# The first k-tile without its norm and shift, and two k-tiles' modulation sums on VectorE, in a two-branch transformer layer

## Chip, cores and metric

The kernel runs on one core of a Trainium2 chip. The metric is the device time of one execution in microseconds; the number given for a kernel is the median of several runs. Profiles are taken of one further execution, whose span is the time from its first to its last instruction.

TensorE multiplies, VectorE and ScalarE do element-wise work, GpSimd (POOL) here mostly issues DMAs, and SyncE (SP) issues nearly all loads. Each engine, and each queue of DMA issues, works through its own list in order.

## The reference, cut to what matters

One layer over 128 context and 256 latent tokens (384 together, three tiles of 128), with a model width of 2048 (16 k-tiles of 128 channels), all in float32:

```python
def modulation(cond, w_mod, b_mod):
    m = jax.nn.silu(cond) @ w_mod + b_mod          # 2048 -> 6 * 2048
    return jnp.split(m[..., None, :], 6, axis=-1)  # sh1, sc1, g1, sh2, sc2, g2

h = rms_norm(x, n1) * (1 + sc1) + sh1
p = h @ w_in                                       # 2048 -> 4096: q, k, v, u
...
x = x + g1 * token_mixing(h, attn, u, ...)         # h again, for the gates
h2 = rms_norm(x, n2) * (1 + sc2) + sh2
x = x + g2 * swiglu(h2, w_gate_up, w_down)
```

Context tokens have one condition vector, latent tokens another, so each channel has two shifts and two scales. The change touches only the way from x to `h @ w_in`.

## The kernel before

**Products.** A float32 product is made of three: each operand is split into a rounded high part H (ScalarE) and the rest L (VectorE), and TensorE adds H·H, L·H and H·L in PSUM. `unit` does so for two k-tiles of a weight chunk of 512 columns (lines 170, 171, 176), and `next_unit` splits the next unit's weights beforehand and then steps the side jobs. A side job is a generator behind a `Paced` object, which takes so many steps per unit as its rate says.

**Input projection.** It needs all 16 k-tiles of h, and each needs its modulation sums, 2.1 MB of weights per k-tile. So it is done in four groups of k-tiles (`GROUPS`): k-tile 0; 1 and 2; 3 to 6; 7 to 15. Each group runs over all eight chunks of 512 columns (`ORDER`), with one accumulator `acc` in SBUF per chunk, to which the later groups are added (`done`, line 783). Group 0 is 24 blocks (eight chunks by three token tiles), with an explicit table `opening_jobs` of what is put beside which block.

**Opening.** The tokens are loaded first, transposed on TensorE (`turn`, line 511), squared on ScalarE; `roots` makes 1/rms from the sums and a row `rB` of it over all partitions. After the tokens come k-tile 0's modulation weights (four loads, lines 419 and 436), then the first weight units. Only when the norm, the scale and the shift are there does `opening_high` make k-tile 0's operand.

**Modulation sums.** `mod_sums` multiplies SiLU(cond) with shift and scale weights, four small products side by side in TensorE's columns (line 436), eight steps per entry (first k-tile, count) of `MODS`, four for a single k-tile. `mod_cols` turns the result (line 452) and makes shift and scale columns; `modulate` makes a k-tile's H and L (scale and shift on ScalarE). `prepare` does this for all entries in turn, paced by `PREP` and `DUE` per group. The weights go through four buffers `wm`, the projection's through four buffers `raw`; both are issued on SP's queue when a buffer is free. `scale` multiplies the other k-tiles by `rB`, one per unit.

**Later.** When `prepare` is done, `with_rows` gives its memory to the modulation rows of the second half, which VectorE sums (line 363) beside the products.

PSUM has four tiles for products in groups 0 to 2 (`ps`) and four for the rest (`pa`); a block or a unit's three token tiles take one each.

## Time and profile before

| | us |
|---|---|
| median of 3 runs (2005.52 to 2007.36) | 2006.64 |
| the profiled execution | 2005.29 |
| its span | 2003.5 |
| TensorE busy | 1989.5 (99% of the span) |
| VectorE busy | 1226.0 (61%) |
| ScalarE busy | 718.3 (36%) |
| first product of the projection (k-tile 0) | starts at 19.66 |
| first product of k-tiles 1 and 2 | starts at 44.82 |
| first product of k-tiles 3 to 6 | starts at 88.56 |
| first product of k-tiles 7 to 15 | starts at 173.53 |

A row of a timeline has the start, the length, the engine, the line and operation, the output and inputs with their shapes, how many instructions were merged, and in brackets how long the engine was idle before and what ended that. Products overlap: one of 512 columns is listed with 0.39 us, but the next starts 0.23 later. A float32 product that is not split is two records in the trace. Rows of groups have minimum, median and maximum of one instruction in ns. Rows of DMA issues have the count, the size of one and the median time from issue to landing.

### The profile page before, as it was taken

What the parts mean: (1) busy time and instruction counts of PE and PEld (TensorE: products, weight loads), DVE (VectorE), ACT (ScalarE), POOL (GpSimd) and SP (SyncE); (2) the same over time, 40 slices, a digit from 0 to 9 for tenths busy, and PEclk for the clock granted to TensorE, in tenths of its full rate; (3) what the DMA queues carried; (4) which work ended last, traced back from release to release, by engine and by line L of the source; (5) the groups of instructions that cost most, each with busy time, mean ns of one, the idle gap of its engine ahead of it and who ended that gap; (6) DMA issues with size and microseconds to landing.
All of it is one profiled execution on the core that took longest, in us unless ns stands there. A gap on an engine that the chain in (4) does not pass through costs nothing.

```text
span 2003.5 us, 24190 instructions
## 1 busy us (share of the span) xinstructions
PE 1989.5 (99%) x9404; PEld 1628.4 (81%) x9404; DVE 1226.0 (61%) x1493; ACT 718.3 (36%) x1052; POOL 73.9 (4%) x106
## 2 busy tenths in 40 slices
PE   8999999999999999999999999999999999999999
PEld 5767888887777888889988888888888888888887
DVE  6745999879877886776843454554334433434654
ACT  6324332445554443344423322323232233223231
POOL 0000010101010100100001000001000000000000
PEclk9999999999999999999999999999999999999999
DMA  9896898888886898764457464547444544455463
GB/s 347 289 342 206 308 288 312 271 278 283 269 255 216 284 330 264 252 231 131 134 182 200 158 189 164 188 139 211 137 150 129 165 153 131 132 152 174 158 185 104
DMA packets 140658, 425.28 MB, mean 212 GB/s; under 512 B 17856, under 2 KB 39296, under 8 KB 139520
## 3 DMA queue, kind: packets, MB, share of 16 engines
q1 hardware_dynamic: 127344, 400.51, 60.4%
q0 software_dynamic: 9600, 16.88, 3.9%
q10 hardware_dynamic: 3600, 6.34, 0.9%
q8 instruction: 74, 1.21, 0.2%
q14 instruction: 40, 0.33, 0.0%
HBM read 387.50 MB, written 44.63 MB: 216 GB/s over the span
## 4 chain that ended last, share of the span: by engine, by line
PE 95%; DMA 2%; DVE 2%; ACT 1%; issue 1%; SPq 0%; DVEq 0%; ACTq 0%
PE mm L170 19%; PE mm L176 18%; PE mm L171 18%; PE at L170 10%; PE at L171 10%; PE at L176 10%; PE at L436 1%; DMA wm<-in_w_mod 1%; PE at L1039 1%; PE at L977 1%; PE at L1056 1%; DVE wl L156 1%; PE at L1447 1%; PE at L1453 1%; PE mm L1453 1%; PE mm L1447 1%
## 5 line engine op out<-in xcount | busy, mean ns | idle before, releaser
L156 DVE TENSOR_TENSOR wl<-wraw,wh 128x1024 fp32r<-128x1024 f32 (+1 forms) x464 | 553.7, 1202 | 435.1 <-ACT wh L155 251.7
L155 ACT CAST wh<-wraw 128x1024 fp32r<-128x1024 f32 (+1 forms) x464 | 478.5, 1038 | 757.9 <-PE mm L171 454.1
L170 PE MATMUL mm<-wh,hH 128*128 128x512 f32 x1316 | 518.2, 394 | 0.3 <-ACT hH L155 0.3
L171 PE MATMUL mm<-wh,hL 128*128 128x512 f32 x1316 | 513.2, 390 | 0.2
L176 PE MATMUL mm<-wl,hH 128*128 128x512 f32 x1316 | 357.2, 389 | 0.2 <-DVE wl L156 0.2
L363 DVE SCALAR_TENSOR_TENSOR accr<-wmr,csz,accr 128x1024 f32<-128x1024 f32 x240 | 301.6, 1278 | 4.6 <-DMA wmr<-in_w_rows 4.6
L170 PEld LDWEIGHTS mm<-wh,hH 128*128 128x128 f32 x1316 | 247.0, 188 | 65.6 <-issue 12.7
L176 PEld LDWEIGHTS mm<-wl,hH 128*128 128x128 f32 x1316 | 246.9, 188 | 52.2 <-DVE wl L156 0.6
L171 PEld LDWEIGHTS mm<-wh,hL 128*128 128x128 f32 x1316 | 247.2, 188 | 50.6 <-DVE hL L156 0.8
L170 PE MATMUL at<-wh,hH 128*128 128x512 f32 x616 | 240.1, 390 | 0.0
L171 PE MATMUL at<-wh,hL 128*128 128x512 f32 x616 | 239.7, 389 | 0.0
L176 PE MATMUL at<-wl,hH 128*128 128x512 f32 x616 | 169.4, 389 | 0.0
L176 PEld LDWEIGHTS at<-wl,hH 128*128 128x128 f32 x616 | 115.6, 188 | 24.0
L171 PEld LDWEIGHTS at<-wh,hL 128*128 128x128 f32 x616 | 115.7, 188 | 23.9
L170 PEld LDWEIGHTS at<-wh,hH 128*128 128x128 f32 x616 | 115.6, 188 | 23.9
L170 PE MATMUL mm<-wh,cH 128*128 128x512 f32 x278 | 108.1, 389 | 0.0
L171 PE MATMUL mm<-wh,cL 128*128 128x512 f32 x278 | 108.1, 389 | 0.0
L176 PE MATMUL mm<-wl,cH 128*128 128x512 f32 x278 | 76.6, 389 | 0.0
L170 PE MATMUL at<-wh,cH 128*128 128x512 f32 x196 | 76.2, 389 | 0.0
L171 PE MATMUL at<-wh,cL 128*128 128x512 f32 x196 | 76.2, 389 | 0.0
L783 DVE TENSOR_TENSOR acc<-acc,mm 128x512 f32<-128x512 f32 x60 | 40.4, 685 | 43.8 <-PE mm L176 43.8
L171 PEld LDWEIGHTS mm<-wh,cL 128*128 128x128 f32 x278 | 52.2, 188 | 10.8
(287 smaller groups left out, 1817.1 us busy)
## 6 DMA issues: line engine op xcount, KB each, us to landing
wraw<-in_w_gate_up SPq DMA_DIRECT2D x176, 512.0 KB, 3.8
wmr<-in_w_rows SPq DMA_DIRECT2D x128, 512.0 KB, 5.2
wraw<-in_w_down SPq DMA_DIRECT2D x88, 512.0 KB, 3.9
wraw<-in_w_gate SPq DMA_DIRECT2D x64, 512.0 KB, 5.0
wraw<-in_w_in SPq DMA_DIRECT2D x60, 512.0 KB, 5.6
wm<-in_w_mod SPq DMA_DIRECT2D x24, 768.0 KB, 6.1
wraw<-in_w_o SPq DMA_DIRECT2D x32, 512.0 KB, 6.2
wm<-in_w_mod SPq DMA_DIRECT2D x28, 512.0 KB, 6.1
```

The source lines that it names most:

```text
L155: nc.scalar.copy(H, x)
L156: nc.vector.tensor_sub(L, x, fr(H))
L170: nc.tensor.matmul(po[t], H[k0 + i][:, sl], wH[:, i], start=first and i == 0, stop=False)
L171: nc.tensor.matmul(po[t], L[k0 + i][:, sl], wH[:, i], start=False, stop=False)
L176: nc.tensor.matmul(po[t], H[k0 + i][:, sl], wL[:, i], start=False, stop=last and i == n - 1)
L363: nc.vector.scalar_tensor_tensor(out=acc[:, cnd], in0=wm, scalar=sc, in1=acc[:, cnd], op0=ALU.mult, op1=ALU.add)
L436: nc.tensor.matmul(pm[q : q + 32, :w], csz[:, k, :], wm[:, kk + par, ty, :], start=k < 2, stop=k >= KT - 2, tile_position=(0, q), skip_gro ...
L783: nc.vector.tensor_add(a, a, po[t])
L977: nc.tensor.matmul(po[j][:, cols], t["q"][rows[j], q], t["k"][rows[j], k], start=True, stop=True, tile_position=(j * HD, 0),)
L1039: nc.tensor.transpose(o[:, i * P : (i + 1) * P], sc[:, j, c0 : c0 + P], ident)
L1447: nc.tensor.matmul(o, a, xH, start=u + kk == 0, stop=False)
L1453: nc.tensor.matmul(o, a, wide(u + kk)[0], start=False, stop=last and kk == 1)
```

## The change

1. *Opening.* The tokens come turned from the host's layout (`x_turned`), so no transposes. First on SP's queue stand the scale half of k-tile 0's weights, that k-tile's tokens and the first two weight units; the shift half and the other tokens follow. Here are rows of SP's queue, before from the eleventh load on, now from the first (`xc`, `xT`: tokens; `wm`: modulation weights; `wraw`: weights of the projection):

```order
L484 DMA xc_133<-in_x_in 128x512
L484 DMA xc_134<-in_x_in 128x512
L419 DMA wm_151<-in_w_mod 128x1024
L419 DMA wm_153<-in_w_mod 128x1024
L419 DMA wm_155<-in_w_mod 128x1024
L419 DMA wm_157<-in_w_mod 128x1024
L228 DMA wraw_159<-in_w_in 128x2x512
```

```order
L490 DMA wm_137<-in_w_mod 128x1024
L490 DMA wm_138<-in_w_mod 128x1024
L485 DMA xT_133<-in_x_turned 128x384
L229 DMA wraw_142<-in_w_in 128x512 x2
L229 DMA wraw_145<-in_w_in 128x512 x2
L490 DMA wm_148<-in_w_mod 128x1024
L490 DMA wm_149<-in_w_mod 128x1024
L485 DMA xT_133<-in_x_turned 128x1152
L485 DMA xT_134<-in_x_turned 128x1536
L229 DMA wraw_154<-in_w_in 128x512 x2
L485 DMA xT_135<-in_x_turned 128x1536
L485 DMA xT_136<-in_x_turned 128x1536
```

Twelve token loads headed the queue before, then k-tile 0's weights; now two loads of scale weights do, and the last tokens are the fourteenth and fifteenth load.

2. *Group 0* multiplies `x * scale` of k-tile 0, not normed and not shifted. When group 1 is added, the accumulator is multiplied by 1/rms per token (`r1`, line 960). The shift's part is a row per condition, shift times weights (`shift_rows`), written to DRAM and, in group 2, loaded to all partitions and added (`shifted`). The operand of k-tile 0 that the gates need later is made at the end of group 2. The squares are summed beside group 0's blocks: ScalarE squares three quarters, VectorE one and folds the others in (`squares`, `fold`), TensorE sums over the partitions (`square_sums`). On TensorE's queue, blocks 15 to 19 now read (`mm`: a block's products; `at`: side work; `sqx`: squares; `ssr`: their sums):

```order
L863 MATMUL mm_379<-wh_338,hH_24_225 128x512
L864 MATMUL mm_379<-wh_338,hL_25_226 128x512
L865 MATMUL mm_379<-wl_339,hH_24_225 128x512
L437 MATMUL at_384<-wm_162,csz 32x256 x4
L863 MATMUL mm_392<-wh_338,hH_24_225 128x512
L864 MATMUL mm_392<-wh_338,hL_25_226 128x512
L865 MATMUL mm_392<-wl_339,hH_24_225 128x512
L437 MATMUL at_384<-wm_164,csz 32x256 x4
L863 MATMUL mm_406<-wh_338,hH_24_225 128x512
L864 MATMUL mm_406<-wh_338,hL_25_226 128x512
L865 MATMUL mm_406<-wl_339,hH_24_225 128x512
L564 MATMUL at_411<-sqx_131,ones 32x384 x4
```

The first step for k-tiles 1 and 2 stood after block 3 before and stands after block 15 now, the square sums after block 17; the eighth step comes after block 21, where it came after block 16; the transposes that follow it came after block 18 and come after block 22 now.

3. *K-tiles 14 and 15.* `MODS` ends at k-tile 13. `last_columns` sums the other two on VectorE: sixteen loads on GpSimd's queue into one buffer, each followed by two passes (line 715), at 0.95 per unit from group 1 on; then one product against ones, a way through DRAM to turn it, and `modulate`. VectorE's queue in group 1, before and now (`acc`: accumulators, `wl`: split weights, `total`: the new sums, `wml`: their weights):

```order
L156 TENSOR_TENSOR wl_692<-wraw_513,wh_691 128x1024
L539 TENSOR_TENSOR xT_136<-xT_136,rB_168 128x384
L783 TENSOR_TENSOR acc_366<-acc_366,mm_688 128x512
L783 TENSOR_TENSOR acc_366<-acc_366,mm_689 128x512
L783 TENSOR_TENSOR acc_366<-acc_366,mm_690 128x512
```

```order
L157 TENSOR_TENSOR wl_696<-wraw_547,wh_695 128x1024
L630 TENSOR_TENSOR xT_134<-xT_134,rB_173 128x384
L715 SCALAR_TENSOR_TENSOR total<-wml_667,csz,total 128x512 x2
L960 SCALAR_TENSOR_TENSOR acc_240<-acc_240,r_172,mm_692 128x512
L960 SCALAR_TENSOR_TENSOR acc_240<-acc_240,r_172,mm_693 128x512
L960 SCALAR_TENSOR_TENSOR acc_240<-acc_240,r_172,mm_694 128x512
```

Two passes that read a loaded buffer now stand ahead of each unit's accumulations.

4. *Pace.* `DUE` and `PREP` for groups 1 and 2 are other numbers, and `prepare` and the shift adds are run to their end where group 3 begins, so `with_rows` comes there.

```diff
-MODS = [(0, 1), (1, 2), (3, 2), (5, 2), (7, 3), (10, 3), (13, 3)]
+MODS = [(0, 1), (1, 2), (3, 2), (5, 2), (7, 3), (10, 3), (13, 1)]
+LAST = (14, 2)
-DUE = [-1.4, 0, 0, 0]
-PREP = [1.75, 2.5, 1.8, 1.8]
+DUE = [-1.4, -1, 0.4, 0]
+PREP = [1.75, 2.8, 1.6, 1.8]
...
-            for t in range(NT):
-                load_tokens(t)
+            wm_scale = load_first(1)
+            load_tokens(0, 0, 1)
+            loads = Ahead(load_unit, units, 2)
+            wm_shift = load_first(0)
+            load_tokens(0, 1, 4)
+            load_tokens(1)
+            loads.more()
+            load_tokens(2)
+            load_tokens(3)
+            loads.more()
             for _ in range(4):
                 src.more()
...
+            def squares(cc):
+                if cc:
+                    nc.scalar.activation(out=sq[1], in_=xT[cc], func=AF.Square)
+                else:
+                    nc.vector.tensor_mul(sq[0], xT[0], xT[0])
+            def fold():
+                nc.vector.tensor_add(sq[0], sq[0], sq[1])
...
+            def shift_rows(j):
+                o = at_tile()
+                for g in range(4):
+                    nc.tensor.matmul(
+                        o[32 * g : 32 * g + 32], sh0, opened[2 * j + g // 2][0][:, g % 2],
+                        start=True, stop=True, tile_position=(0, 32 * g), skip_group_check=True,
+                    )
+                row = tmp.tile([P, CH], F32, tag="junk", bufs=1, name=nm("srow"))
+                nc.scalar.copy(row, o)
+                for g in range(4):
+                    nc.gpsimd.dma_start(s_shift[j][2 * g : 2 * g + 2], row[32 * g : 32 * g + 2])
...
+            def last_columns():
...
+                def load(k):
+                    wm = tmp.tile([P, 2 * n * P], F32, tag="junk", bufs=1, name=nm("wml"))
+                    nc.gpsimd.dma_start(wm, io[f"w_mod{kt0}"][:, k].rearrange("p i n -> p (i n)"))
+                    return wm
+                wm = load(0)
+                yield
+                for k in range(KT):
+                    for cnd in range(2):
+                        a, sc = total[:, cnd], csz[:, k, cnd : cnd + 1]
...
+                            nc.vector.scalar_tensor_tensor(
+                                out=a, in0=wm, scalar=sc, in1=a, op0=ALU.mult, op1=ALU.add
+                            )
+                    if k < KT - 1:
+                        wm = load(k + 1)
+                    yield
...
+            last = Paced(last_columns(), 0.95)
...
             def opening_high():
                 for c, sl in conds2:
-                    nc.vector.tensor_scalar(
-                        h0H[:, sl], xT[0][:, 0, sl], msc[0][:, 0, c : c + 1], msh[0][:, 0, c : c + 1],
-                        op0=ALU.mult, op1=ALU.add,
-                    )
+                    nc.vector.tensor_scalar_mul(h0H[:, sl], xT[0][:, 0, sl], msc[0][:, 0, c : c + 1])
...
             opening_jobs = [
                 (1, 1, lambda: open_pair(1, 0)),
                 (3, 1, lambda: open_pair(1, 1)),
+                (4, 1, shift_sums),
+                (5, 1, warm_sqrt),
+                (6, 1, shift_columns),
+                (7, 1, lambda: squares(0)),
+                (8, 1, lambda: shift_rows(0)),
...
+                (12, 1, fold),
...
+                (14, 1, fold),
+                (15, 1, step),
+                (15, 1, lambda: squares(3)),
...
+                (16, 1, fold),
+                (16, 1, step),
+                (17, 1, square_sums),
...
+                (21, 2, step),
+                (22, 3, step),
+                (23, 2, step),
...
                         def done(t):
                             a = acc[ci][:, t]
-                            nc.vector.tensor_add(a, a, po[t])
+                            if gi > 1:
+                                nc.vector.tensor_add(a, a, po[t])
+                                return
+                            nc.vector.scalar_tensor_tensor(
+                                out=a, in0=a, scalar=r1[:, t : t + 1], in1=po[t], op0=ALU.mult, op1=ALU.add
+                            )
```

More of the change, by code (lines that the diff above doesn't have):

```diff
@@ L516, in square @@
-            def square(t, cc):
-                junk = tmp.tile([P, CH], F32, tag="junk", bufs=1, name=nm("junk"))
-                nc.scalar.activation(
-                    out=junk, in_=xc[cc][:, t], func=AF.Square, accum_out=ssx[:, t, cc : cc + 1]
-                )
+            pick = tmp.tile([P, 2], F32, tag="pick", bufs=1, name="pick")
+            nc.vector.tensor_reduce(
+                out=pick, in_=ident.rearrange("p (a c) -> p c a", c=32)[:, 0:2], axis=AX.X, op=ALU.add
+            )
@@ new lines, in picked @@
+            def picked(o, mrow, w=P):
+                for t in range(w // P):
+                    nc.tensor.matmul(
+                        o[:, 2 * t : 2 * t + 2], mrow[:, t * P : (t + 1) * P], pick, start=True, stop=True
+                    )
+                return o[:, : 2 * (w // P)]
+            def squares(cc):
[3 more added lines that the diff above has]
+                    nc.vector.tensor_mul(sq[0], xT[0], xT[0])
@@ new lines, in fold, with square_sums @@
+            def fold():
+                nc.vector.tensor_add(sq[0], sq[0], sq[1])
+            norm = {}
+            def square_sums():
+                pm = at_tile()
+                for k in range(4):
+                    q = 32 * k
+                    nc.tensor.matmul(
+                        pm[q : q + 32, :TOK], ones, sq[0][:, k], start=True, stop=True,
+                        tile_position=(0, q), skip_group_check=True,
+                    )
+                norm["row"] = tmp.tile([P, CH], F32, tag="junk", bufs=1, name=nm("ssr"))
+                nc.scalar.copy(norm["row"][:, :TOK], pm[:, :TOK])
@@ L522, in roots, with roots_row @@
             def roots():
-                nc.vector.tensor_reduce(out=ss1, in_=ssx, axis=AX.X, op=ALU.add)
-                for _ in inv_sqrt(r1, ss1, D, [P, NT]):
+                ss = picked(at_tile(), norm["row"], TOK).rearrange("p (t c) -> p t c", c=2)[:, :, 0]
+                for _ in inv_sqrt(r1, ss, D, [P, NT]):
                     pass
+            def roots_row():
                 o = at_tile()
@@ L572, in trunk_kernel @@
             sums = []
-            for i, _ in enumerate(mod_sums(src, *MODS[0], wme, sums)):
-                if i == 5:
-                    roots()
-                    unread(1)
-            unread(2)
-            loads.more()
-            loads.more()
-            prepared = [1]
-            cols = mod_cols(*MODS[0], sums.pop())
-            next(cols)
-            unread(5)
-            for _ in cols:
-                pass
+            prepared = [1]
+            unread(10)
+            o = picked(at_tile(), first_sums(wm_scale, 3))
+            unread(3)
+            nc.vector.scalar_tensor_tensor(
+                out=msc[0][:, 0], in0=o, scalar=b0[:, 0:1], in1=ng[:, 0, 0:1].to_broadcast([P, 2]),
+                op0=ALU.add, op1=ALU.mult,
+            )
             def columns_and_tokens(k0, n):
@@ L648, in open_pair @@
                 split(H[:, j], L[:, j], raw[:, j])
-                if j:
-                    loads.more()
             opening_high()
@@ L729, in with_rows @@
                 behind.append(rows)
-            prep.then = with_rows
-            behind += [scales, prep]
+            behind += [scales, prep, last]
             def after(ci):
@@ L768, in trunk_kernel @@
                 prep.least = 3.6 if gi > 1 else 1
+                if gi == 2:
+                    shift = Paced(shifted())
+                    behind.append(shift)
                 if gi == len(GROUPS) - 1:
+                    shift.drain()
+                    behind.remove(shift)
+                    prep.drain()
+                    with_rows()
+                    last.rate = 1
                     behind.append(Paced(head_constants(), 0.2))
```

173 lines of the change are left out of this document (130 added, 43 removed).

## The prediction

> **What bounds the kernel now.** I read the page's busy lines first, then the chain, then what TensorE waited for in the first 200 us, because every edited line runs before 180 us.
>
> ```profile
> PE 1989.5 (99%) x9404; PEld 1628.4 (81%) x9404; DVE 1226.0 (61%) x1493; ACT 718.3 (36%) x1052; POOL 73.9 (4%) x106
> PE 95%; DMA 2%; DVE 2%; ACT 1%; issue 1%; SPq 0%; DVEq 0%; ACTq 0%
> PE at L511 <- DMA xc<-in_x_in: 3.8, 1, 3.8
> PE at L436 <- DMA wm<-in_w_mod: 3.1, 5, 0.7
> PE mm L170 <- ACT hH L155: 0.3, 1, 0.3
> ```
>
> TensorE is the bound from end to end. Time can be won in two ways only: its first product starts earlier, or it gets less to do. Either counts only if nothing that feeds it becomes late. Now the opening (timelines; the columns are start, length, engine, line):
>
> ```profile
> 3.82 2.79 PE L511 MATMUL at<-ident,xc 128*128 128x128 f32 x12 [3.82 <-DMA xc<-in_x_in]
> 6.42 0.63 ACT L518 ACTIVATE junk<-xc 128x512 f32<-128x512 f32 x1 [0.18 <-DMA xc<-in_x_in]
> 13.40 0.65 PE L436 MATMUL at<-wm,csz 128*32 128x128 f32 x16 [0.65 <-DMA wm<-in_w_mod]
> 17.14 0.64 PE L436 MATMUL at<-wm,csz 128*32 128x128 f32 x16
> 17.72 0.71 PE L570 MATMUL mm<-ident 128*128 128x128 f32 x4
> 17.86 0.27 ACT L444 COPY mrow<-at 128x128 f32<-128x128 f32 x1 [0.36 <-PE at L436]
> 19.16 0.67 DVE L623 TENSOR_SCALAR hH<-xT,ms 128x128 fp32r<-128x128 f32 x2
> 19.66 1.03 PE L689 MATMUL mm<-wh,hH 128*128 128x512 f32 x3
> 10.00:20.00 10.00, 7.94 (x102) 5.78 (x102) 6.35 (x19) 7.01 (x18) 0.00 (x0) 1.00 1.04 404
> 20.00:30.00 10.00, 10.00 (x63) 5.78 (x63) 6.83 (x12) 5.67 (x11) 0.00 (x0) 1.00 1.03 401
> ```
>
> The reader should see that the first real product waits until 19.66 for bytes: 3.1 MB of tokens and 2.1 MB of modulation weights at about 400 GB/s. The rows also give a landing curve: the fourth quarter-MB (1.05 MB) is there at 6.42, 3.67 MB at 13.40, and from there 0.40 MB per us.
>
> **The change, part by part.** *Start.* Only the scale half of k-tile 0's weights (1.05 MB) stands ahead of the first product. It lands at about 6.4 by the curve. Then come half of L436's last 32 records (0.6; 16 cost 0.64), and the way from their end (17.72, where L570 starts) to the product at 19.66, which is 1.9, less two of three small VectorE steps (0.2 each): 1.55. First product at 8.5, so 11.1 us earlier.
>
> *What k-tile 0's blocks then carry.* The prices, and the block's end before:
>
> ```profile
> 30.66 0.39 PE L696 MATMUL mm<-wh,hH 128*128 128x512 f32 x1
> 31.35 0.39 PE L696 MATMUL mm<-wh,hH 128*128 128x512 f32 x1
> 32.83 0.64 PE L436 MATMUL at<-wm,csz 128*32 128x256 f32 x8 [0.63 <-DMA wm<-in_w_mod]
> 33.40 0.50 PE L696 MATMUL mm<-wh,hH 128*128 128x512 f32 x1
> 39.99 0.38 PE L452 MATMUL at<-ident,mrow 128*128 128x128 f32 x2
> 43.74 1.07 PE L436 MATMUL at<-wm,csz 128*32 128x256 f32 x16
> 44.26 0.51 ACT L155 CAST hH<-hf 128x384 fp32r<-128x384 f32 x1
> 44.82 0.50 PE L170 MATMUL mm<-wh,hH 128*128 128x512 f32 x1
> ```
>
> A block of three products is 0.69 us, so 24 are 16.5, and 0.3 more for the first three. Nine modulation steps (eight records of 256 columns, 0.6 each) are 5.4, transposes 0.3. New on TensorE: the shift sums, 32 records, two times 0.6 = 1.2; the two shift rows, each eight records of 512 columns, twice the 256-column step, 1.0 each = 2.0; the square sums (384 columns) 0.75; picks and the transposes of r 0.5. That is 4.4 us of new work which stood under the loads before or did not exist. Without waits the first product of k-tiles 1 and 2 would come at 8.5 + 16.8 + 5.4 + 0.3 + 4.4 = 35.4.
>
> *Waits there.* Three, each from a queue. (1) The first weights of k-tiles 1 and 2 now stand behind 7.3 MB on SP's queue and end at 7.86 MB: 13.4 + 4.19/0.40 = 23.8, while TensorE has block 15 behind it at 8.5 + 0.3 + 16 x 0.69 + 1.2 + 1.0 = 22: 1.9 us. (2) The squares. A VectorE pass over 128x1536 is taken as 1.75 us, from 128x512 at 0.68 and 128x1024 at 1.22:
>
> ```profile
> L156 DVE TENSOR_TENSOR wl<-wraw,wh x35: 681/1219/1226, 19.7 to 175.5; 128x1024 fp32r<-128x1024 f32 x27, 128x512 fp32r<-128x512 f32 x8
> ```
>
> From block 7's end (8.5 + 0.3 + 8 x 0.69 + 1.2 = 15.5) VectorE has one square and three folds (7.0), four splits (about 2.6) and five accumulator copies (0.6 to 0.7 each), and it runs through them back to back to 28.2; the sums over them are reached by TensorE at 23.8 + 2 x 0.6 + 2 x 0.69 = 26.4: 1.8 us. (3) The weights of steps 6 to 8 have their buffers free only as steps 2 to 4 end, some 0.4. And k-tiles 1 and 2 become operands late: transposes, three small steps, scaling and rounding need at least 2.7 us from transpose to product, and only one block and one step (1.3) stand between them now, where five blocks and two steps stood (39.99 to 44.82): 1.1 us rounded down. Together 5.2. Bounds: 0, if the loads come at a higher rate from the first byte (they also shorten VectorE's queue), and 9, if (1) and (2) add up with later loads. I take 5.2, the queue as it stands.
>
> So k-tiles 1 and 2 start at 40.6 instead of 44.82, with one step fewer behind them (0.6): 3.6 us won, not 11.1.
>
> *K-tiles 14 and 15.* The later stretches start and end here:
>
> ```profile
> 88.56 0.39 PE L170 MATMUL mm<-wh,hH 128*128 128x512 f32 x1
> 157.43 2.79 PE L436 MATMUL at<-wm,csz 128*32 128x384 f32 x32
> 173.53 0.39 PE L170 MATMUL at<-wh,hH 128*128 128x512 f32 x1
> ```
>
> Eight units of k-tiles 1 and 2 run from 44.82 to 88.56, 5.47 us each; sixteen of 3 to 6 from 88.56 to 173.53, 5.31 each. The last three k-tiles took eight steps of 0.70 to 0.75, 6.0 with gaps; one k-tile takes four of 0.65, 2.6. Two transposes fall (0.25); two sums against ones and one transpose come (0.75). Net 2.9 us off TensorE.
>
> *What VectorE takes instead.* 32 passes of 128x512, 16 pairs. The nearest row is a 128x1024 pass of the same form:
>
> ```profile
> L363 DVE SCALAR_TENSOR_TENSOR accr<-wmr,csz,accr x240: 1268/1278/1284, 196.7 to 1354.9; 128x1024 f32<-128x1024 f32 x120
> 56.37 0.69 DVE L783 TENSOR_TENSOR acc<-acc,mm 128x512 f32<-128x512 f32 x1 [0.67 <-PE mm L176]
> 56.98 1.22 DVE L156 TENSOR_TENSOR wl<-wraw,wh 128x1024 fp32r<-128x1024 f32 x1
> 58.11 0.55 DVE L539 TENSOR_TENSOR xT<-xT,rB 128x384 f32<-128x384 f32 x1
> 59.81 0.69 DVE L783 TENSOR_TENSOR acc<-acc,mm 128x512 f32<-128x512 f32 x1 [1.15 <-PE mm L176]
> ```
>
> A pair is about 1.3 us, and the gap ahead of an accumulation is 1.15: as work it fits. The shift adds (0.7 + 1.2 per chunk) go beside two units of 3 to 6. Not the work but its wait is the question. Each pair reads one buffer that only the pair before frees: pair, load by GpSimd's queue, pair. That is a loop of 1.3 us plus the landing, and behind the waiting pair in VectorE's queue stand the accumulations that free PSUM and the splits for TensorE. Paced at 0.95 per unit, a pair is due every 5.76 us first, and every (84.97 - 2.9)/16/0.95 = 5.4 later. No such load is in the trace; the nearest:
>
> ```profile
> wraw<-in_w_in SPq DMA_DIRECT2D x8, 256.0 KB, 4.6
> s_gate<-gst ACTq DMA_DIRECT2D x24, 256.0 KB, 5.4
> s_sum<-s_sum POOLq DMA_DIRECT2D x8, 256.0 KB, 7.0
> s_row<-in_b_mod POOLq DMA_DIRECT2D x16, 4.0 KB, 3.9
> ```
>
> Bounds 3.9 (same queue, hardly any bytes) and 7.0 (same bytes, but added into DRAM). I take 4.6, a plain load of the same 256 KB. The loop is then 5.9: 0.14 late seven times, 0.5 nine times, 5.5 us. TensorE tolerates about 4 (of four PSUM tiles three are in use, so an accumulation may come two thirds of a unit late, and the next split is one unit ahead). Cost 1.5.
>
> [...]
>
> **Sum.** Profiled execution 2005.29 (span 2003.5): -3.6 - 2.9 + 1.5 = -5.0, so 2000.3; that execution lies 1.35 under the median, so 2001.6 as a median.
>
> **Rivals.** *The loop binds (slower).* With 5.4, the 256 KB row on a queue of its own, the period is 6.7: 7 x 0.94 + 9 x 1.3 = 18.3, less 4: 14.3 instead of 1.5, so 2014. It breaks even at a landing of 4.9. For it: the loaded rows and DMA at 0.9 or more of its time in the opening. Against it: a longer period also thins the traffic, and other loads land sooner then. [...]
>
> *The opening keeps its lead.* None of the 5.2 us is waited: 1996.4. For it: the token rows that set my curve are short pieces, the new first loads longer ones. Against it: VectorE's queue holds (2) in any case.
>
> *The opening's lead is lost.* DMA has to feed k-tiles 1 and 2 faster (2.8 steps per unit where 2.5 were), and the 3.6 go in waits there; only 2.9 less 1.5 is left: 2005.2, nothing that can be measured.
>
> **Chances.** A measurement of this kernel can tell about 0.2% (4 us) from no change. Forecast 0.45 (own range 1997 to 2006), loop binds 0.22, lead kept 0.17, lead lost 0.16. Faster than 2002.6: 0.6 of the first, all of the third, 0.2 of the fourth: 0.48. Slower than 2010.6: most of the second, 0.19. The rest 0.33. The range 1995 to 2012 leaves out the far half of the loop and the edge of the lead kept.
>
> **What would show it.** First product at 8 to 9 us; the k-tiles' second group at 40 to 42; its third group's start 5 us before 88.56, and the last group's 5 before 173.53. In TensorE's waits, the first 256-column step on its weights and the square sums on VectorE, near 2 us each. The load for pair k landing in 4.6 us. Wrong, if VectorE idles on that load by more than 1 us a unit (the loop), or if TensorE has no wait in the blocks (the lead kept).

## The result

The changed kernel takes 2060.59 us (median of five runs, 2052.47 to 2060.82), the kernel before, timed beside it, 2005.52 (2005.26 to 2007.36): a ratio of 1.0257, interval 1.0236 to 1.0278. It is 2.6% slower, where 2001.6 was forecast with a range that ended at 2012. The profiled execution took 2052.47 (two of the five runs took 2052.5, three 2060.7); its span is 2050.7, and against the span of 2003.5 before, 47.2 us have been lost.

Where, is read from the first product of each stage on TensorE, the first copy of a gate product to `gst`, and the first load of a finished gate from `s_gate` (times in us from the start of the span; the page calls VectorE DVE and ScalarE ACT; in `unit` the lines now stand one higher, L171, L172 and L177):

| stretch | before | after | lost |
|---|---|---|---|
| start to k-tile 0 | 19.66 | 9.09 | -10.6 |
| k-tile 0's products and what is beside them | 25.16 | 41.39 | +16.2 |
| k-tiles 1 to 6 (first product 44.82; 50.48) | 128.71 | 158.53 | +29.8 |
| k-tiles 7 to 15 (173.53; 209.01) | 180.02 | 187.65 | +7.6 |
| attention and gate (353.55; 396.66) | 296.40 | 300.28 | +3.9 |
| all behind (649.95; 696.94) | 1353.55 | 1353.76 | +0.2 |

The busy line and the chain from the page of the changed kernel:

```profile
PE 2003.3 (98%) x9408; PEld 1634.3 (80%) x9408; DVE 1261.1 (61%) x1538; ACT 716.1 (35%) x1037; POOL 96.9 (5%) x149
PE 84%; DVE 7%; DMA 5%; issue 2%; ACT 1%; POOL 0%; DVEq 0%; SPq 0%; ACTq 0%
```

TensorE's share of the chain has gone from 95 to 84%, VectorE's from 2 to 7. And TensorE is busy for 13.8 us longer, although the sums of two k-tiles are gone from it. Its waits in the first 300 us (total, times, longest):

```profile
PE mm L171 <- DVE acc L958: 13.0, 5, 3.5
PE at L564 <- DVE sqx L556: 7.0, 1, 7.0
PE mm L171 <- DVE acc L960: 4.3, 3, 3.4
PE mm L171 <- ACT hH L156: 2.7, 2, 2.3
PE at L171 <- DVE ms L460: 1.8, 1, 1.8
PE at L437 <- DMA wm<-in_w_mod: 1.2, 1, 1.2
```

The opening first (timeline: start, length, engine, line; in brackets the idle time ahead and who ended it):

```profile
9.09 0.95 PE L856 MATMUL mm<-wh,hH 128*128 128x512 f32 x3
22.79 1.75 DVE L556 TENSOR_TENSOR sqx<-sqx,sqx 128x1536 f32<-128x1536 f32 x1
24.59 0.64 PE L437 MATMUL at<-wm,csz 128*32 128x256 f32 x8 [1.16 <-DMA wm<-in_w_mod]
24.63 1.49 ACT L551 ACTIVATE sqx<-xT 128x1536 f32<-128x1536 f32 x1 [1.99 <-issue]
26.48 0.62 ACT L156 CAST wh<-wraw 128x512 fp32r<-128x512 f32 x1
27.14 0.69 DVE L157 TENSOR_TENSOR wl<-wraw,wh 128x512 fp32r<-128x512 f32 x1 [1.99 <-ACT wh L156]
27.75 1.75 DVE L556 TENSOR_TENSOR sqx<-sqx,sqx 128x1536 f32<-128x1536 f32 x1
29.58 1.48 ACT L551 ACTIVATE sqx<-xT 128x1536 f32<-128x1536 f32 x1 [2.48 <-issue]
32.70 1.75 DVE L556 TENSOR_TENSOR sqx<-sqx,sqx 128x1536 f32<-128x1536 f32 x1
34.59 1.51 PE L564 MATMUL at<-sqx,ones 128*32 128x384 f32 x8 [7.01 <-DVE sqx L556]
50.48 0.50 PE L171 MATMUL mm<-wh,hH 128*128 128x512 f32 x1 [2.34 <-ACT hH L156]
```

The three folds start 4.95 us apart. ScalarE squares each quarter into the one buffer `sq[1]`, so its square at 24.63 starts only when the fold of 22.79 has read that buffer. Behind the square, in ScalarE's order, stand a copy and the rounding of the next weights (26.48); VectorE's split of these weights (27.14) has waited 1.99 us for the rounding, and the next fold stands behind the split. So the chain runs from fold to square (1.5 us), copy, rounding, split and fold (1.75 us), and VectorE is idle in it, though it has work in its queue. Behind the 7 us wait TensorE runs at half speed (the same eight modulation records that took 0.64 take 1.11 at 35.85). The windows show it; the last figures are granted clock, DMA share and GB/s:

```profile
20.00:30.00 10.00, 6.42 (x36) 3.40 (x34) 6.79 (x8) 5.54 (x8) 1.35 (x3) 1.00 1.03 407
30.00:40.00 10.00, 5.41 (x34) 2.64 (x35) 3.19 (x5) 3.12 (x5) 0.00 (x0) 0.66 0.23 66
```

DMA nearly stands still there too (its share is 0.23): TensorE's products free the weights' buffers, and SyncE's issues wait for them, the longest 9.8 us. Then k-tiles 1 to 6, in two windows each (the two groups). Before:

```profile
44.80:88.50 43.70, 42.53 (x262) 29.90 (x261) 32.06 (x51) 14.54 (x22) 0.00 (x0) 1.00 0.91 319
88.50:173.50 85.00, 85.00 (x488) 59.30 (x487) 42.13 (x59) 29.12 (x44) 0.00 (x0) 1.00 0.78 285
```

And after:

```profile
50.40:102.60 52.20, 47.41 (x272) 32.91 (x272) 38.70 (x61) 15.68 (x24) 3.10 (x6) 0.93 0.86 315
102.60:209.00 106.40, 91.48 (x488) 63.75 (x489) 69.26 (x96) 26.75 (x41) 15.05 (x29) 0.92 0.72 250
```

Of the 29.8 us lost, TensorE is idle for 18.5 (19.7 against 1.2), and busy for 11.4 longer over the same products: the clock is granted at 0.93 and 0.92, where it was 1.00. (TensorE's clock is at half for 23.9 of the 158.5 us, and half of that is 11.9.) VectorE is busy for 108 of 158.6 us, so it has room on average. What it waits for (0 to 300 us):

```profile
DVE total L715 <- DMA wml<-in_w_mod: 19.1, 7, 4.7
DVE acc L617 <- DMA shb<-s_shift: 10.1, 4, 3.9
DVE acc L616 <- DMA shb<-s_shift: 2.5, 4, 1.0
```

Both kinds of load are GpSimd's (`wml`: a pair's weights; `shb`: a chunk's two shift rows). Their issues with the median us to landing, and one turn on the timelines of GpSimd, VectorE and TensorE:

```profile
wml<-in_w_mod POOLq DMA_DIRECT2D x16, 256.0 KB, 4.7
shb<-s_shift POOLq DMA_DIRECT2D x16, 256.0 KB, 5.4
```

```profile
137.89 0.54 POOL L704 DMA_DIRECT2D wml<-in_w_mod  x1 [9.40 <-DVE total L715]
138.42 1.06 POOL L609 DMA_DIRECT2D shb<-s_shift  x2
140.93 1.42 DVE L715 SCALAR_TENSOR_TENSOR total<-wml,csz,total 128x512 f32<-128x512 f32 x2 [2.20 <-DMA wml<-in_w_mod]
142.63 0.69 DVE L616 TENSOR_TENSOR acc<-acc,shb 128x512 f32<-128x512 f32 x1 [0.28 <-DMA shb<-s_shift]
147.20 1.23 DVE L617 TENSOR_TENSOR acc<-acc,shb 128x1024 f32<-128x1024 f32 x1 [3.88 <-DMA shb<-s_shift]
149.08 0.50 PE L171 MATMUL mm<-wh,hH 128*128 128x512 f32 x1 [2.57 <-DVE acc L958]
```

GpSimd could not issue the pair's load until VectorE had done the pair before it (9.40 us), and the two shift loads stood behind that issue. VectorE then waits for three loads in a row, the accumulator adds stand behind it, and TensorE has no PSUM to go on with.

### The profile page after: what moved, and what is told of

It reads as the page before. It is cut to its first block, busy times and chain, and to the rows that moved or that the text cites. A ratio compares the mean times of both kernels' runs of the same rounds, so it can differ in the third digit from the quotient of the medians.

```text
span 2050.7 us, 24351 instructions
## 1 busy us (share of the span) xinstructions
PE 2003.3 (98%) x9408; PEld 1634.3 (80%) x9408; DVE 1261.1 (61%) x1538; ACT 716.1 (35%) x1037; POOL 96.9 (5%) x149
## 4 chain that ended last, share of the span: by engine, by line
PE 84%; DVE 7%; DMA 5%; issue 2%; ACT 1%; POOL 0%; DVEq 0%; SPq 0%; ACTq 0%
PE mm L171 17%; PE mm L177 16%; PE mm L172 16%; PE at L177 9%; PE at L171 9%; PE at L172 9%; DVE accr L364 2%; DVE wl L157 2%; DMA shb<-s_shift 2%; DMA wm<-in_w_mod 1%; DVE acc L958 1%; PE at L1156 1%; PE at L1218 1%; PE at L1235 1%; DMA wml<-in_w_mod 1%
## 5 line engine op out<-in xcount | busy, mean ns | idle before, releaser
L171 PE MATMUL mm<-wh,hH 128*128 128x512 f32 x1316 | 523.4, 398 | 20.0 <-DVE acc L958 13.0
L172 PE MATMUL mm<-wh,hL 128*128 128x512 f32 x1316 | 517.5, 393 | 1.7 <-DVE hL L157 1.6
L177 PE MATMUL mm<-wl,hH 128*128 128x512 f32 x1316 | 361.6, 393 | 2.2 <-DVE wl L157 2.2
L171 PEld LDWEIGHTS mm<-wh,hH 128*128 128x128 f32 x1316 | 249.4, 189 | 87.6 <-DVE acc L958 15.2
L177 PEld LDWEIGHTS mm<-wl,hH 128*128 128x128 f32 x1316 | 250.0, 190 | 56.3 <-DVE wl L157 3.4
L172 PEld LDWEIGHTS mm<-wh,hL 128*128 128x128 f32 x1316 | 249.7, 190 | 53.1 <-DVE hL L157 2.9
L171 PE MATMUL at<-wh,hH 128*128 128x512 f32 x616 | 240.2, 390 | 1.9 <-DVE ms L460 1.8
L172 PE MATMUL at<-wh,hL 128*128 128x512 f32 x616 | 239.7, 389 | 0.0
L177 PE MATMUL at<-wl,hH 128*128 128x512 f32 x616 | 169.6, 389 | 0.6 <-DVE wl L157 0.6
L171 PEld LDWEIGHTS at<-wh,hH 128*128 128x128 f32 x616 | 115.6, 188 | 26.7 <-issue 2.2
L177 PEld LDWEIGHTS at<-wl,hH 128*128 128x128 f32 x616 | 115.4, 188 | 25.2 <-DVE wl L157 1.3
L172 PEld LDWEIGHTS at<-wh,hL 128*128 128x128 f32 x616 | 115.6, 188 | 23.9
L171 PE MATMUL mm<-wh,cH 128*128 128x512 f32 x278 | 108.1, 389 | 0.0
L172 PE MATMUL mm<-wh,cL 128*128 128x512 f32 x278 | 108.1, 389 | 0.0
L177 PE MATMUL mm<-wl,cH 128*128 128x512 f32 x278 | 76.7, 389 | 0.0
L171 PE MATMUL at<-wh,cH 128*128 128x512 f32 x196 | 76.2, 389 | 0.0
L172 PE MATMUL at<-wh,cL 128*128 128x512 f32 x196 | 76.2, 389 | 0.0
L171 PEld LDWEIGHTS mm<-wh,cH 128*128 128x128 f32 x278 | 52.2, 188 | 10.8
L177 PEld LDWEIGHTS mm<-wl,cH 128*128 128x128 f32 x278 | 52.2, 188 | 10.8
```

Source lines behind the costliest of these rows:

```text
L171: nc.tensor.matmul(po[t], H[k0 + i][:, sl], wH[:, i], start=first and i == 0, stop=False)
L172: nc.tensor.matmul(po[t], L[k0 + i][:, sl], wH[:, i], start=False, stop=False)
L177: nc.tensor.matmul(po[t], H[k0 + i][:, sl], wL[:, i], start=False, stop=last and i == n - 1)
```

## Experiments

Each kernel is timed against the kernel before; the diffs are against the changed kernel unless another is named.

**1. Two loads ahead.** Each pair's weights go into one of two buffers of their own, so that two pairs' loads are under way.

```diff
-                wm = load(0)
+                ahead = [load(0), load(1)]
...
+                    wm = ahead.pop(0)
...
-                    if k < KT - 1:
-                        wm = load(k + 1)
+                    if k < KT - 2:
+                        ahead.append(load(k + 2))
```

> The weights of k-tiles 14 and 15 for VectorE are loaded two pairs ahead into memory that their own operands use later (two loads of 128 KB per pair instead of one of 256 KB); nothing else changes. Theory (the loop pair-load-pair through one buffer stalls VectorE's queue, 19.1 us of waits for wml in the changed kernel's trace): those waits fall under 4 us and the time by 12 to 20 us, to about 2040 to 2048. Rival (VectorE has too much work in groups 1 and 2, the waits are only where it shows): the waits move to other rows and the time falls by under 5 us.

Measured 2049.93, ratio 1.0215 (1.0198 to 1.0232): some 8 us gained by the two ratios, where 12 to 20 were expected. The waits on `wml` are gone; those on the shift loads rise from 12.6 to 22.8:

```profile
DVE acc L616 <- DMA shb<-s_shift: 17.8, 5, 5.1
DVE acc L617 <- DMA shb<-s_shift: 5.0, 4, 3.1
```

The loop is real, but it is not alone: one kind of load takes the other's place.

**2. Sums back on TensorE.** K-tiles 14 and 15 go through TensorE as before; opening and shift rows stay.

```diff
-MODS = [(0, 1), (1, 2), (3, 2), (5, 2), (7, 3), (10, 3), (13, 1)]
-LAST = (14, 2)
+MODS = [(0, 1), (1, 2), (3, 2), (5, 2), (7, 3), (10, 3), (13, 3)]
...
```

> All modulation sums of norm 1 on TensorE as before, the new opening and the shift rows stay. Theory (two thirds of the loss lie in what VectorE waits for in groups 1 and 2, the opening costs about 6): TensorE gets 2.9 us back to do, the wml waits are gone, the shift rows' 12.6 us of waits stay: 2025 to 2035. Rival (the opening alone is what costs, by its late start and what follows): over 2045. Rival (without VectorE's sums the opening wins): under 2003.

Measured 2030.82, ratio 1.0113 (1.0098 to 1.0128). K-tiles 1 to 6 take 130.4 us again (before 128.7), so the sums on VectorE are what costs there. The waits on the shift loads, expected to stay at 12.6, fall to 2.3 with no pair's load ahead of them on GpSimd's queue. But k-tiles 7 to 15 still take 189.7, and the opening ends at 55.3. TensorE's waits to 300 us, and two stretches of that opening:

```profile
PE at L563 <- DVE sqx L555: 7.4, 1, 7.4
PE at L170 <- ACT wh L155: 4.8, 1, 4.8
```

```profile
35.00:40.00 5.00, 4.54 (x27) 1.72 (x27) 0.92 (x2) 1.00 (x2) 0.00 (x0) 0.50 0.19 41
40.00:45.00 5.00, 5.00 (x29) 2.71 (x25) 1.51 (x6) 0.27 (x2) 0.00 (x0) 0.50 0.70 277
```

**3. No shift rows.** The loads and adds of the shift rows are left out.

```diff
                 for n, ci in enumerate(ORDER):
-                    load(n)
                     yield
-                    a = acc[ci]
-                    nc.vector.tensor_add(a[:, 0], a[:, 0], got[n][0])
...
                     yield
```

> Leaves out the loads of the shift rows from DRAM and their addition to the accumulators (the shift's part is missing from the input projection). Theory (12.6 us of VectorE's waits for shb in group 2, each ahead of the accumulations, in the same queue as the wml loads): the time falls by 10 to 18 us, and the wml waits in group 2 shrink too, since two loads fewer stand on GpSimd's queue. Rival (the wml loop sets the pace by itself): under 5 us.

Measured 2045.9, ratio 1.0185 (1.0165 to 1.0205). Now the pair's waits rise, from 19.1 to 28.8, where they were expected to shrink. What experiment 1 showed from one side shows from the other.

**4. Squares in buffers of their own.** The third and fourth quarter's squares are written to four free tiles each.

```diff
-                if cc:
+                if cc > 1:
+                    kts = range(4 + 2 * cc, 6 + 2 * cc)
+                    own[cc] = [hpool.tile(...) for kt in kts for x in "HL"]
+                    for k in range(4):
+                        nc.scalar.activation(out=own[cc][k], in_=xT[cc][:, k], func=AF.Square)
+                elif cc:
...
```

> Squares of the third and fourth quarter get buffers of their own (in memory that later operands use), by 384 columns instead of 1536, so ScalarE need not wait for the fold before. Theory (the 7.0 us that TensorE waits for the square sums come from ScalarE and VectorE taking turns on one buffer): that wait falls to 1 to 3 us, the first product of k-tiles 1 and 2 comes 4 to 6 us earlier than 50.5, and the time falls by as much. Rival (the wait is VectorE's amount of work beside the blocks): the wait stays above 5.

Measured 2049.89, ratio 1.0202 (1.0184 to 1.0219). The wait for the squares falls from 7.0 to 2.9, and the opening ends at 47.22: the single buffer is the cause of 4.1 of the 7.0 us. K-tile 7 starts at 207.91, though, 1.1 earlier and not 3.3; the load loops behind take the rest. The median is some 11 us below the changed kernel's, more than was expected, but the profile doesn't show where: its span, 2051.8, is as long.

**5. Sums on VectorE alone.** The kernel before, with its opening, and only k-tiles 14 and 15 as in the change.

```diff
-MODS = [(0, 1), (1, 2), (3, 2), (5, 2), (7, 3), (10, 3), (13, 3)]
+MODS = [(0, 1), (1, 2), (3, 2), (5, 2), (7, 3), (10, 3), (13, 1)]
+LAST = (14, 2)
...
+                    prep.drain()
+                    with_rows()
+                    last.rate = 1
...
```

> The opening is the one before; only the sums of k-tiles 14 and 15 go to VectorE, and the rows start at the third group's first product as in the change. Theory (each part costs on its own: pair, load and pair follow each other through one buffer): k-tiles 1 and 2 start at 44.8 as before; VectorE waits 20 to 30 us on these loads (28.8 without the shift loads on the queue), TensorE some 15 of it, and the third group costs 8 and attention 4 as in every kernel so far: 2028 to 2036. Rival 1 (the loads only collide with the shift rows' on GpSimd's queue): waits below 5 us, 2012 to 2018, the third group's 12 alone. Rival 2 (the third group's loss comes from the new opening): third group as before, 180 us.

Measured 2036.66, ratio 1.0144 (1.0127 to 1.0161). K-tiles 1 to 6 take 151.1, 22.4 more than before, with no shift load in the kernel at all:

```profile
DVE total L638 <- DMA wml<-in_w_mod: 32.7, 10, 6.9
```

So the single buffer of the pair is enough by itself to make VectorE wait. Rival 1 falls. K-tiles 7 to 15 take 184.2 and attention 300.4, where 180.0 and 296.4 stood before: 4 us each, where 8 and 4 were expected. The new opening isn't in this kernel, so rival 2 falls.

**6. Rows started as before.** Experiment 2, with the rows of the later modulations again behind the end of the preparation instead of behind a drain.

```diff
+            prep.then = with_rows
...
-                    prep.drain()
-                    with_rows()
```

> The kernel with all sums on TensorE (2030.8), and the rows of the later modulations start when the last k-tile is prepared, as before, instead of at the third group's first product behind a drain of what is left of the preparation. Theory (the third group and attention lose time because the preparation is drained and the rows start there, which shifts VectorE's row work onto the group's own): third group 189.7 to some 180, attention about 3 us less: 2017 to 2022. Rival (VectorE is late there for another reason, the drained shift rows or the start of the group): no gain, 2028 to 2032.

Measured 2038.88, ratio 1.0153 (1.0138 to 1.0169): 8 us worse, not 10 better, and outside both ranges. K-tiles 7 to 15 take 187.1 instead of 189.7, but what lies behind attention takes 1368.3 instead of 1353.6. The next kernel has the same trouble and shows it more plainly.

**7. Opening mended.** Experiments 4 and 6 together, and the square sums two blocks and two modulation steps later.

```diff
-                (17, 1, square_sums),
                 (17, 1, step),
...
+                (19, 1, square_sums),
...
```

> All sums on TensorE, rows as before, squares in buffers of their own, and the square sums two blocks and two modulation steps later (2.6 us of work ahead of them). Theory (the 7.4 us wait is squares through one buffer, and the half clock of 30 to 47 us follows from the idle time): wait below 1 us, no stretch of clock under 0.9 between 30 and 50 us, k-tiles 1 and 2 start at 43 to 46 instead of 55.3, total 9 to 12 below the kernel with rows as before: 2006 to 2012. Rival (the loads of the next steps then bind, and groups 1 and 2 eat the gain as they did with the squares' buffers alone): start at 46 to 48, total 2014 to 2018.

Measured 2028.04, ratio 1.0104 (1.0089 to 1.0119). The opening does nearly what was expected: no wait for the squares, clock 1.00 in every stretch from 25 to 40 us (then 0.93, and 0.73 from 45 to 50, behind a wait of 2.35 us ahead of k-tiles 1 and 2), k-tiles 1 and 2 at 43.27, k-tile 7 at 172.39, 1.1 ahead of the kernel before. The total does not: of 23.7 us lost against it in the span, 6 lie in k-tiles 7 to 15, and most of the rest in two waits on one line, the longer one at 887 us:

```profile
PE at L398 <- DMA colr<-s_row: 13.7, 1, 13.7
PE at L398 <- ACT pt L1166: 3.0, 1, 3.0
```

L398 turns the columns of a later modulation, which are ready when its rows are. Here the first row pass stands behind 41 weight splits in VectorE's order, before the change behind 39; in the changed kernel behind 35. Of all the kernels here, only the two with 41 (experiments 6 and 7) wait for the column on L398.

**8. No waits on GpSimd's loads.** Experiments 1 and 3 together.

```diff
-                wm = load(0)
+                ahead = [load(0), load(1)]
...
-                    load(n)
                     yield
-                    a = acc[ci]
...
                     yield
```

> The changed kernel with the loads of the VectorE sums two pairs ahead and without the shift rows' loads and adds (the shift of norm 1 is left out of the output). Theory (the waits on GpSimd's loads are the loss of groups 1 and 2; VectorE's work in them fits beside TensorE): no wait over 1 us on these loads, groups 1 and 2 together 126 to 130 us instead of 158.5: 2020 to 2028. Rival (VectorE's added passes themselves make it late): waits gone, groups 1 and 2 still 140 or more: 2034 to 2042.

Measured 2032.23, ratio 1.0127 (1.0112 to 1.0142). VectorE waits for neither load, and k-tiles 1 to 6 take 134.2: of the 29.8 us lost there, 24.3 go with these waits (and with the shift adds, which are gone as well). The other 5.5 stay although TensorE has less to do, so neither the theory's 126 to 130 nor the rival's 140 holds: TensorE is idle for 5.0 us, against 1.2 before, and at half clock for 6.8.

**9. Pace as before.** Experiment 7 with the preparation's old pace, which puts the first row pass behind 39 splits again.

```diff
-DUE = [-1.4, -1, 0.4, 0]
-PREP = [1.75, 2.8, 1.6, 1.8]
+DUE = [-1.4, 0, 0, 0]
+PREP = [1.75, 2.5, 1.8, 1.8]
```

> The mended opening with all sums on TensorE, and the preparation paced as before the change (2.5 and 1.8 steps per unit, no offsets) instead of 2.8 and 1.6, so that the first row pass stands behind 39 splits of weights, as before, and not behind 41. Theory (in the last kernel rows that start two units later made the transpose of the late column wait 13.7 us, and lost some 6 in the third group): that wait gone, third group 180 to 181 us, third group's start 172 to 173: 2002 to 2006. Rival (the wait comes from the load of that column itself, behind other loads on its queue): wait stays 10 us or more, 2022 to 2028.

Measured 2007.63, ratio 1.0006 (0.9997 to 1.0015), a little over the range. The wait at L398 is gone, k-tiles 7 to 15 take 180.0, attention 298.5. The pace, which moves the rows by two places in VectorE's order, was worth 20 us; k-tiles 1 to 6, where the pace itself acts, take as long with either (129.6 and 129.1). The opening's gain (k-tile 7 at 171.91 instead of 173.53) is used up in attention, and the kernel is as fast as before.

**10. First split earlier.** The same, with the split of the first weights of k-tiles 1 and 2 at block 19 instead of 21.

```diff
                 (19, 1, square_sums),
+                (19, 1, split_unit),
...
-                (21, 1, split_unit),
```

> The same, and the split of the first weights of k-tiles 1 and 2 moved from block 21 to block 19, out of the way of the three small steps that make the columns (they waited for it from 39.6 to 41.1). Theory: wait before the first product of k-tiles 1 and 2 falls from 2.35 to about 1 us, start 1.2 us earlier, total 1 us below the other one. Rival (the split holds up the squares' sums or the accumulator copies instead): no gain or a loss of 1 us.

Measured 2007.73, ratio 1.0008 (0.9998 to 1.0017): no gain. The wait for the late operands falls from 1.26 to under 0.3, k-tiles 1 and 2 start at 42.56 instead of 42.33. But in this profile the first product came 1.27 us later (10.24 instead of 8.97), so counted from there the opening is 1.0 shorter, as was expected; k-tiles 1 and 2 then take 2.0 us longer, with a wait of 1.88 for weights of a modulation step where it was 1.04.

**11. Rows at the group's start.** Experiment 9, with the drain and the rows where the change has them.

```diff
-            prep.then = with_rows
...
+                    prep.drain()
+                    with_rows()
```

> The mended opening with all sums on TensorE at the pace of before (2007.6), and one thing taken over from the change: the rest of the preparation is drained at the third group's first product and the rows start there, behind 35 splits instead of 39. Theory (the drain and the early row passes make the split of the group's weights late; with all sums on TensorE it cost 9.7 in the third group and 2.7 in attention): third group 188 to 190 instead of 180, attention 2 longer, 2016 to 2021. Rival (the third group's loss comes from what groups 1 and 2 leave late, not from this order): third group 180 to 182, 2006 to 2009.

Measured 2020.12, ratio 1.0063 (1.0046 to 1.0079). K-tiles 7 to 15 take 190.5 instead of 180.0, attention 301.3 instead of 298.5. The two longest of TensorE's waits, one in each stretch (at 184 and 451 us):

```profile
PE at L170 <- ACT wh L155: 4.8, 1, 4.8
PE at L1165 <- DVE sc L1152: 4.6, 1, 4.6
```

The drain and the early rows are the third cause of the loss; they cost without the old waits of the opening and without the sums on VectorE.

**12. Mended, with the sums on VectorE.** Experiment 9 with experiment 1's sums, rows started at the third unit of k-tiles 7 to 15.

```diff
+LAST = (14, 2)
...
+                        if gi == len(GROUPS) - 1 and ci == ORDER[0] and u == k0 + 4:
+                            prep.drain()
+                            with_rows()
...
+                ahead = [load(0), load(1)]
```

> The mended opening and pace (2007.6), rows started at the third unit of the third group, and the sums of k-tiles 14 and 15 on VectorE with their loads two pairs ahead: the whole change with every wait mended that was found. Theory (the passes themselves delay the splits and the accumulator adds behind them: without any wait on loads groups 1 and 2 still took 134.2 us against 129.1 with the sums on TensorE): 2011 to 2018. Rival (VectorE has room, and 2.9 us of TensorE's work is won): 2003 to 2005.5.

Measured 2043.74, ratio 1.0179 (1.0156 to 1.0201), worse than either theory. VectorE's waits on the shift loads, with two pairs' loads under way and a mended opening:

```profile
DVE acc L629 <- DMA shb<-s_shift: 12.1, 4, 3.8
DVE acc L630 <- DMA shb<-s_shift: 11.1, 5, 3.8
```

**13. Shift loads first.** Experiment 12, with the shift step ahead of the pair's step in each unit, so that GpSimd has its loads ahead of the weight loads that wait for a pair.

```diff
-                    behind.append(shift)
+                    behind.insert(0, shift)
```

> The mended kernel with the sums of k-tiles 14 and 15 on VectorE (2043.7), and one thing else: in each unit of k-tiles 3 to 6 the shift step comes ahead of the pair's step, so that the two shift loads stand on GpSimd's queue ahead of the weight loads that wait for the pair of the same unit, and not behind them. Theory (GpSimd's queue in order: the shift loads, 23 us of waits, are issued only when the pair before them in the program is done): waits on shift loads 23 to below 6 us, groups 1 and 2 from 155 to some 135 to 140, total 2018 to 2028. Rival (their landing, over 5 us for 256 KB, is too long for one unit of 5.3 us wherever they stand): waits stay over 15 us, 2038 to 2046.

Measured 2029.71, ratio 1.0109 (1.0094 to 1.0124). The order on the queue was most of it (7.0 us of waits stay where below 6 was expected, and the total lies just above its range):

```profile
DVE acc L629 <- DMA shb<-s_shift: 5.2, 3, 2.3
DVE acc L630 <- DMA shb<-s_shift: 1.8, 2, 1.2
```

K-tiles 1 to 6 take 140.1 us instead of 155.1. They are still 10.6 longer than with the sums on TensorE (experiment 9), k-tiles 7 to 15 6.5 and attention 4.3. What does that was not taken apart: in the latter two it can be VectorE's passes or the rows' start, which here stands behind 38 splits and a drain.

**14. The changed kernel with that line alone.**

```diff
-                    behind.append(shift)
+                    behind.insert(0, shift)
```

> The changed kernel (2060.6) with that order alone. Theory (two causes, the queue's order for the shift loads and the single buffer for the pair's load): shift waits from 12.6 to below 4 us, the pair's own waits stay near 19 or rise as without the shift rows (28.8), total 2045 to 2053, as the kernel without any shift loads (2045.9). Rival (order does not matter): 2058 to 2062.

Measured 2045.38, ratio 1.0194 (1.0175 to 1.0213): some 13 us by the two ratios, for one moved line; in the profiles k-tiles 1 to 6 are 10.9 shorter. The shift waits fall to 1.3, the pair's stay as they were:

```profile
DVE total L715 <- DMA wml<-in_w_mod: 20.2, 8, 5.1
DVE acc L617 <- DMA shb<-s_shift: 1.3, 1, 1.3
```

**15. Idle time filled.** The changed kernel, with unread products in the wait for the square sums.

```diff
+                (17, 1, lambda: unread(54)),
                 (17, 1, square_sums),
```

> The changed kernel, with 54 small products that nobody reads (128 columns, about 0.12 us each, 6.3 us) in the 7.0 us in which TensorE waits for the square sums. Theory (TensorE's granted clock falls because it stands idle): granted clock 0.95 or more from 30 to 45 us where it was 0.66, the products behind the square sums at 0.23 us a step and not 0.43, k-tiles 1 and 2 at 48 to 49 us instead of 50.5; the total moves by 2 us or less, since the load loops behind bind. Rival (the clock falls for another reason, such as the load's own power): clock and start as before.

Measured 2055.28, ratio 1.0242 (1.0224 to 1.026). The products took 12.2 us, not 6.3 (each is two records), so the start, at 53.69, cannot be compared. The clock can:

```profile
27.39 12.22 PE L653 MATMUL mm<-ident 128*128 128x128 f32 x108
39.53 0.85 PE L564 MATMUL at<-sqx,ones 128*32 128x384 f32 x8
```

```profile
35.00:40.00 5.00, 5.00 (x50) 4.69 (x52) 0.37 (x1) 0.00 (x0) 0.00 (x0) 1.00 0.00 0
50.00:55.00 5.00, 2.66 (x14) 1.03 (x12) 2.78 (x6) 3.66 (x9) 0.59 (x1) 0.84 0.99 358
```

Without idle time the clock stays at 1.00 and the square sums take 0.85 where they took 1.51; it falls again only behind the next wait, the 2.34 us ahead of k-tiles 1 and 2. So the idle time is the cause of the half speed there.

## Why the prediction was wrong

The sign was missed. Two steps failed: the wait for the squares, priced as one queue's work, and above all VectorE's loop, where 1.5 us stood against a loss of 29.8 in its stretch; a third cause, the drain and the rows' start, was in no step. One by one:

- *First product at 8.5.* It came at 9.09, and in the fourteen other kernels with this opening between 8.94 and 10.24. About right, with the landing curve it was read from.
- *Wait (1), 1.9 us for the first weights.* 1.16. Right in kind. The size is partly luck: TensorE got there at 23.43 and not at 22, and the weights landed at 24.59 and not at 23.8.
- *Wait (2), 1.8 us for the squares.* 7.01. This step failed. It summed VectorE's work from block 7's end and let it run back to back to 28.2; the last fold ended at 34.45. VectorE was idle for 5.1 us on the way, in three waits for ScalarE's rounding of weights, which stands behind the squares; two of these squares wait for the fold before. So the wait came out 5.2 longer. The work was counted, and the shared buffer and ScalarE's order were not. Experiment 4 gave the squares buffers, and 4.1 us of the wait went; experiment 7, which also puts the sums later, took the rest.
- *Wait (3), 0.4 for the weights of later steps.* TensorE's rows show none.
- *Late operands, 1.1.* 2.34 and 0.35: the lower bound was taken as the value. Experiment 10 shows one more part of it, the split in VectorE's queue: moving it takes 1.0 or more off the 1.26 that are left in experiment 9.
- *K-tiles 1 and 2 at 40.6.* 50.48. Of the 9.9 us, 0.6 come from the first product, 5.3 from the waits (1.16, 7.01 and 2.34 instead of 5.2), and 1.8 from the half clock: square sums, a modulation step and a block behind them took 0.66, 0.50 and 0.65 longer than in experiment 15. Most of the remaining 2.2 is a term that was left out: a block behind a modulation step or other side work lasts 0.8 to 0.95 (0.90 from 25.16 to 26.06), not 0.69, and there are some ten. The waits' bounds of 0 and 9 did not hold 10.5.
- *K-tiles 14 and 15, 2.9 us less on TensorE.* It cannot be read off here, as the clock covers it; experiment 8, with all waits on loads mended, loses 5.5 in the same stretch. An estimate that counts TensorE's busy time there in full, and half of it while the clock is at half, gives 126.0 in experiment 8 and 127.6 before, so 1.6 less work.
- *VectorE's loop, 1.5 us.* The term that decides: 29.8 us were lost where 1.4 were to be won (2.9 less 1.5). The landing was sized well, 4.6 against a median of 4.7. What failed is the step from it to the cost, in three places. The added GpSimd work was priced as one loop, though the change also puts 16 shift loads on the same queue behind the loads that wait for a pair; the text put those adds "beside two units" as work. Experiments 13 and 14 price that order at 13 to 14 us. A single landing time was used for all pairs: the changed kernel's landed in 2.9 to 7.7 us, and in experiment 5, which has no shift loads, ten pairs waited 32.7. And TensorE's tolerance of 4 us was taken off the sum of all late pairs once; the trace shows eight separate waits on accumulators, 17.3 together.
- *What no step had.* These waits are paid again in clock: 11.4 us of longer busy time in k-tiles 1 to 6. And there is the drain with the rows' start (11.5 in k-tiles 7 to 15 and attention; experiment 11 gives 13.3 for it alone). It stands in the diff in two lines, `prep.drain()` and `with_rows()`, and the prediction took every edited line to run before 180 us.

Of the rivals, *the loop binds* had the right sign and mechanism. Its price, 14.3, was for that loop only, and low for it too: the sums alone, with no shift load in the kernel, cost 22.4 in k-tiles 1 to 6 (experiment 5). *The opening's lead is lost* was right for the opening, but for the squares, not for DMA, whose share fell to 0.23 there. *The opening keeps its lead* could be had in part: with its waits mended (experiment 9) the opening is 2.5 us ahead at k-tile 1, where 3.6 was forecast, and 1.6 at k-tile 7. That best version equals the kernel before. And with the sums on VectorE, the best version (experiment 13) is still some 22 us longer; the stretches that lose it are known, the causes only in part.

## What to carry to other kernels

When work moves to an engine with room, follow its loads and not its busy time. Here one buffer made a chain of load and use (32.7 us of VectorE's waits in experiment 5), and the shift loads, issued by the same engine behind the waiting load, joined that chain (12.6 us of waits in the changed kernel), which one moved line undid (1.3 in experiment 14). Do the same for two engines that hand one buffer back and forth (a wait of 7.0 us in the opening, 2.9 with buffers of their own in experiment 4). Look through the diff for lines that only shift when a later stage's background work starts: here a pace that started the rows two weight splits later cost 20 us, most of it 680 us later.

## What was not expected of the hardware

TensorE's clock answers to waits shorter than was thought of. Behind the 2.34 us wait ahead of k-tiles 1 and 2 the granted clock fell to 0.84 and then 0.50 (50 to 55 and 55 to 60 us in experiment 15). The clock records of the changed kernel's trace show more. In them the clock is either full or half, and it changes on a grid of 3.41 us. The step of the grid that holds this wait, and the next:

```profile
48.59:52.00 3.41, 1.08 (x3) 0.46 (x3) 1.50 (x5) 3.03 (x7) 0.58 (x1) 1.00 0.97 345
52.00:55.41 3.41, 3.41 (x8) 2.48 (x9) 2.81 (x4) 1.77 (x2) 0.00 (x0) 0.50 1.03 384
```

TensorE was busy for 1.08 of the 3.41 us, and the next 3.41 had half the clock. Counted over the traces of the kernel before and the changed one: at full clock, all 9 steps with TensorE busy for less than 46% were followed by half clock, and none of the 1156 with more than 67%; of the 8 between, 1 was. Of the 10 steps at half clock, all in the changed kernel, the 7 fully busy ones and one busy for 89% were followed by full clock, those busy for 10 and 73% were not. The wait of 2.57 us that ends at 149.08 is longer than the one of 2.34, but it falls across two steps (from 144.16 and from 147.57), busy for 2.35 and 1.91 us, and neither was followed by half clock. So in this trace a wait cost clock or not by where it fell on the grid and what other gaps shared its step.

How long the half clock lasts differs too. Behind the 7.01 us wait of the changed kernel it lasted 6.83 us (31.52 to 38.35), with TensorE busy for a tenth of the first step and all of the second. In experiment 2, behind a wait of 7.43, the clock was 0.57, 0.50, 0.50 and 0.72 in the four windows from 30 to 50 us, some 17 us at half, although TensorE was busy for 9.54 of the 10 us from 35 to 45. The kernels with the same opening differ in it: from 20 to 60 us the clock is at half for some 10 to 14 us in the three with k-tiles 1 and 2 at 50.5 to 51.1 (the changed kernel, experiments 1 and 14), and for some 17 to 19 in the four with them at 54.1 to 55.3 (experiments 2, 3, 6 and 8). What decides between the two was not tried.
